# Modulation vectors as row sums on VectorE in a two-block fp32 kernel

## The chip, the cores and the metric

The kernel runs on one core of a Trainium2 chip. The metric is the device time of one execution in microseconds (us), taken as the median of several runs. TensorE (PE; PEld is its weight load) does matrix products, VectorE (DVE) and ScalarE (ACT) elementwise work, GpSimd (POOL) elementwise work and DMA issues, SyncE (SP) DMA issues alone. Each engine works through its own queue in order.

## The reference, cut to what matters

Two transformer-like blocks run one after the other on 256 latent tokens, the first (two layers) beside 256 context tokens, with features D = 1024. Each layer scales and shifts its normalised input by "modulation" vectors, which come from one condition vector through a matrix of 1024 x 6144:

```
s_lat = silu(c);  s_ctx = silu(c_ctx)                  # each [1024]
for l in range(2):
    ml = split(s_lat @ w_ada[l] + b_ada[l], 6)         # six vectors of 1024
    mc = split(s_ctx @ w_ada[l] + b_ada[l], 6)         # the same for the context
    hl = rmsnorm(xl, g) * (1 + ml[1]) + ml[0]          # needed first of all
    hc = rmsnorm(xc, g) * (1 + mc[1]) + mc[0]
    yl, yc = mixer(hl, hc)     # four mLSTM heads, eight differential attention heads, Fourier, gates
    xl = xl + ml[2] * yl       # from here on the other vectors
    xl = xl + ml[5] * swiglu(rmsnorm(xl, g2) * (1 + ml[4]) + ml[3])
    ...                        # the context likewise, in layer 0
```

The second block (HGRN2 and S5 mixers, then a product-key expert layer) has one such matrix too, `ada_w_2`, and one stream, `silu(c_2)`.

## The kernel before

**Products.** Activations are kept transposed, features on the 128 partitions and tokens along the row (512 columns: latent and context). A product in fp32 is made of three matmuls with operands split into a high and a low part: hi x hi, hi x lo, lo x hi (L217 to L219 for most products, L417 to L419 in `first_products`). The weights arrive by DMA as tiles of 128x1024 (`raw`), ScalarE casts the high part (`whi`, L171 or L189), VectorE takes the difference as the low part (`wlo`, L176 or L190; GpSimd in some products). Two products' worth of weights are in buffers, so the weights of one product are made ready during the one before.

**Work beside the products.** Attention steps, gates and the like are generators. `spend`, called at every product, takes one step of the first generator in `k.todo` (by `fill`) and, by a clock of estimated us, steps of those in `k.bg` (by `tick`):

```
    def fill(self):
        if self.todo:
            if next(self.todo[0], None) is None:
                self.todo.pop(0)
    ...
    def spend(self, us):
        self.fill()
        self.clock += us
        while self.clock >= self.step:
            self.clock -= self.step
            self.tick()
```

Inside the stretches that are scheduled by hand, which hold the modulation, the order on each engine is the order in which the program is written, that is, the order in which these steps are taken; each engine's queue is then fixed.

**Modulation before.** `ada_cond` (L274) makes `cs`, the silu of both conditions as columns [128, 8, 32]; a second one for block 2. `rounds` (L2075, in `block1`) puts six rounds for each of the three matrices into `k.todo`, 18 in all. A round (`ada_round`, L293) makes one vector of 1024 for its streams: for each of eight k it loads a tile of 128x1024 through SP's queue (L304, two buffers with the tag `ada`; the next load is issued in the step that uses the tile two before it), and lets it run through TensorE in four matmuls of 256 columns against `cs[:, k]` (L318, `pada<-ada,cs`). Then the row of results is copied (L323), turned into columns by two transposes (L326) and added to the bias (L335), which gives `ada` [128, streams, 48]. The first two vectors of layer 0, shift and scale of the first norm, are made together in two half rounds from sixteen loads each into buffers with the tag `yb` (L310).

**The start.** `first_products` (L400) makes the first norm and the first five products by halves of the features: k steps 0 to 3 of `affine_steps` (L428: `k`, L437, on VectorE; `h`, L450, on ScalarE; its low part, L452, on VectorE), then the products with these, then steps 4 to 7 and the products with those. Before each half, `mod` (L1043) makes `modA` from that half's modulation. `fill` is called beside the first half's products, and between the halves and after the second `fill_until(16)` empties `k.todo` down to 16 rounds.

Names in the rows: `pacc`, `ps`, `po`, `pada` are PSUM tiles, `x` the residual, `po` in L437 the rows of 1/rms, `e`, `den` attention scores and their row sums, `junk` a tile that nobody reads.

Of the kernel before, what the change touches and what calls it, by code (L numbers as in the profile page):

```python
# [13 lines left out]
AF = mybir.ActivationFunctionType  # L14
ALU = mybir.AluOpType
# [4 lines left out]
for _p, _t in {  # L20
    "C1": "ada adarow c_cosT c_sinT c_dft1 c_dftc c_dfts c_maskf c_maskb dakl craw1 craw2 cth",
    "P1": "q k v oth hn crow cdiag aT e0 e1 ropea ropeb gc h gb gb2 den den2 dast",
    "Y": "yb",
    "Rx": "x",
    "R2": "xl hl",
    "P2": "u",
}.items():
    for _n in _t.split():
        POOL_OF[_n] = _p
# [7 lines left out]
# products between two steps of the work beside them, by length: mLSTM, differential attention, Fourier  # L37
# [12 lines left out]
class K:  # L50
    def __init__(self, tc, d, ctx):
        self.tc, self.nc, self.d, self.ctx = tc, tc.nc, d, ctx
        self.pools = {}
        self.n = 0
        self.guards = {}
        self.bg = []
        self.clock, self.step = 0.0, 2.6
        self.todo = []
        self.ahead = []
        self.lines = None, None  # L60
        # whether GpSimd makes the low parts of the weights of a line
        self.spare = False
        # whether the steps beside a product come before its matrix products in the order, or after them
        self.early = False
# [18 lines left out]
    # ---- work that runs beside the products: generators, one step at a time between product tiles  # L83
# [3 lines left out]
    def tick(self):  # L87
        """one step of the first generator, and of those behind it that it lets start"""
# [29 lines left out]
    def pipe(self, rows):  # L118
        """rows of stages, each row one step behind the row before; the successor starts after the last row's first"""
# [6 lines left out]
    # ---- sections in the order given: the weights of each product are made ready during the one before  # L126
# [4 lines left out]
    def line(self, src, kt, product, after=None, us=0.0, split=False):  # L131
        """product(weights) comes with the next call; after(its result) one call later, in two parts (before and after
        the next weights, or half of them)"""
# [15 lines left out]
    def prepare(self, src):  # L149
        """the weights of the next line before its time"""  # L150
# [14 lines left out]
    # ---- products: every float32 operand is hi + lo, both float32r  # L165
# [30 lines left out]
    def gemm_t(self, acc, src, xs, cols, kt=KT):  # L196
        """acc[n, tok] = sum over k of w[k, n] x[k, tok]"""
        self.gemm_ts([(acc, src)], xs, cols, kt)

    def gemm_ts(self, jobs, xs, cols, kt=KT):  # L200
        """the same for several tiles, k by k: for an x that is still being made"""
# [19 lines left out]
    def gemm_m(self, accs, src, xs, tts):  # L221
        """[tok, 256 cols] = sum over k of x[k, tok] w[k, n], for the token tiles tts, two to a bank of accs;
        the first start of a bank clears it for both"""
# [14 lines left out]
    # ---- constants  # L238
# [13 lines left out]
    def more_consts(self):  # L252
# [16 lines left out]
        # low part of k of one head of the differential attention, for each map with zeros in the other map's rows  # L269
# [3 lines left out]
    # ---- modulation: silu(c) @ w + b, as one column of six vectors for each stream  # L273
# [11 lines left out]

    def ada_tile(self, name, bias, ns):
# [6 lines left out]
    def ada_round(self, cs, w, r, bt, out, ns, half=None):  # L293
        """columns r*1024 .. r*1024+1023 of the modulation, or the same half of each of its first two vectors;
        loads run as far ahead as there are buffers"""
        nc = self.nc
        wts = []

        def load():
            k = len(wts)  # L300
            if k < KT:
                if half is None:
                    wt = self.t([P, 1024], "ada", 2)
                    nc.sync.dma_start(wt, w[k * P:(k + 1) * P, r * 1024:(r + 1) * 1024])  # L304
                    wts.append((wt[:, :T2], wt[:, T2:]))
                else:
                    wts.append([self.t([P, T2], "yb", self.nyb) for _ in range(2)])
                    for v, wt in enumerate(wts[-1]):
                        c = v * 1024 + half * T2
                        nc.sync.dma_start(wt, w[k * P:(k + 1) * P, c:c + T2])  # L310

        for _ in range(2 if half is None else KT):
            load()
        yield "-"
        acc = self.ps("ada")
        for k in range(KT):
# [3 lines left out]
            load()  # L320
# [7 lines left out]
        def part(a):  # L328
            if half is None:
                return a[:, r * 8:(r + 1) * 8].rearrange("p (r j b) -> p r j b", r=2, j=2)  # L330
# [6 lines left out]
    # ---- rmsnorm over the features of x[k] = [128, tok]  # L337
    def sq_add(self, k, src, n, first=None, engine=None):
        """adds the squares of x[k] (and of x[k] * first beside them) to the sums over k"""
# [11 lines left out]
    def sq_cols(self, nt):  # L351
        """the sums over all features, tokens on partitions, a column for each 128"""
# [12 lines left out]
    def rows(self, rs, nt, tag="o", between=None):  # L365
        """columns of tokens to rows on every partition"""
# [8 lines left out]
    def halves(self, srcs):  # L375
        """the weights of pairs of products, first all those of the first half of the features, then of the second"""
# [23 lines left out]
    def first_products(self, accs, split, x, pr, mod, streams):  # L400
        """the first norm and the first products with it, by halves of the features: the second half of its modulation is
        made beside the products with the first. mod(half) gives A, B"""
# [25 lines left out]
    def affine_steps(self, x, pr, A, B, streams, pair, hs, early=0, ks=range(KT)):  # L428
        """x * pr * A + B, split; streams: [(columns, s)] with A[s], B[s] = [128, 8];
        one k a step, the first early of them begun before the first"""  # L430
# [25 lines left out]
    def sq_rows(self, nt, tag="o", work=None, between=None):  # L456
        """1 / rms of the tokens in rows"""
# [7 lines left out]
    # h = x * A / rms + B still lacks the rms when the first products with it are due: these take x * A instead,  # L465
    # with B in a further column: (w^T (x * A)) / rms + w^T B
# [11 lines left out]
    def raw_product(self, w, xs, tags, at=None, between=None):  # L478
        """one tile for each stream that has a tag"""
# [14 lines left out]
    def raw_finish(self, accs, rows, t, bias=True):  # L494
        """acc * rows + w^T B into t; without bias the columns w^T B are returned instead of added"""
# [12 lines left out]
    def norm_ahead(self, base, residual, x, A, B, srcs, tags, norm, finish, rpair, pair, at, follow, after_that,  # L508
                   first=None, close=None):
        """base: the products that end x, [(weights, kt, product, us)], with residual(k, acc); the squares of x are summed  # L510
        on the way, and norm = (columns, rows of 1 / rms). Beside that go the products of srcs with x * A, which
        finish(j, accs, rows) ends; follow() starts the next line, and the weights of the one after that are made ready.
        Returns h"""
# [42 lines left out]
        # h takes the place of x * A  # L556
# [15 lines left out]
    def follow(self, src):  # L572
        """the weights for the first product after a line"""
# [4 lines left out]
    # pairs (high, low) of split activations; with b further columns for each stream  # L578
# [18 lines left out]
    # ---- mLSTM  # L597
    def ml_gates(self, l, acc):
# [10 lines left out]
        # log sigmoid(f) = min(f, 0) - log1p(exp(-|f|)); log1p(e) = 2 atanh(e / (2 + e))  # L609
# [16 lines left out]
        # cumulative sums and maxima in each direction  # L626
# [30 lines left out]
    def ml_qkv(self, l, h, hs, need_ctx, qk):  # L657
        """q^T, k^T [128, 2, tok] and v [tok, 4, 256] of one head; qk: those made already"""
# [21 lines left out]
    def ml_o(self, l, h, hs, th):  # L680
        """tanh(o / 2) of one head"""
# [6 lines left out]
    def ml_head(self, l, h, qkv, th, g, tts, ys):  # L688
# [65 lines left out]
        # y = hn^T * g * (tanh(o/2) + 1); g holds head_g / 2  # L754
# [13 lines left out]
    def av(self, st, nk, vof, w, out):  # L768
        """stages of out[tok, w] = rmsnorm over w of A[tok, nk] @ v, with A = st["A"]"""
# [25 lines left out]
    # ---- differential attention  # L795
# [1454 lines left out]
```

## Time and profile before

| | |
|---|---|
| runs of the kernel before | 3129.56 us median of 3 (3129.42 to 3132.8) |
| the profiled execution | span 3129.0 us (the page gives no other time for it) |
| PE busy | 97% of the span |
| PEld busy | 86% |
| DVE busy | 62% |
| ACT busy | 43% |
| POOL busy | 14% |
| DMA | 153 GB/s in the mean |

The page divides the span among engines. TensorE is busy nearly throughout; whether another engine has room is a question of the stretch, so the rows further below are by stretch and by place.

### The profile page before, as it was taken

The page shows a single profiled execution, that of the slowest core. Times are in us where ns is not written, and L with a number is a line of the kernel's source. Part 1 is how long each engine was busy: PE and PEld are TensorE (multiplying, and loading weights), DVE is VectorE, ACT ScalarE, POOL GpSimd, SP SyncE. Part 2 cuts the span into 40 slices and gives each one's busy share as a digit, 9 for nine tenths or more (in the row PEclk, how much of TensorE's full clock was granted, in tenths as well). Part 3 has the DMA queues.
Part 4 walks back from the last instruction along what each step waited for, and adds up shares of the span by engine and source line. Part 5 has one row for each costly group of instructions (what it writes and reads, how often), then busy time and mean ns, then how long its engine had stood idle before and what let it go on. Part 6 is the DMA issues. An engine that isn't in the chain of part 4 may idle for free.

```text
span 3129.0 us, 53569 instructions
## 1 busy us (share of the span) xinstructions
PE 3036.7 (97%) x21466; PEld 2686.8 (86%) x21466; DVE 1940.2 (62%) x3643; ACT 1350.2 (43%) x2310; POOL 435.8 (14%) x524
## 2 busy tenths in 40 slices
PE   7999999999999999999999999997899999999998
PEld 4778777887787777788898999986799999999998
DVE  5544627653455333474568667689789778866665
ACT  3343425542233221344456545455554545444444
POOL 2101001101121000022001022684210000000000
PEclk9999999999999999999999999998999999999999
DMA  7443343324434434443242355552357765566665
GB/s 257 130 130 118 122 135 121 109 75 128 152 122 135 151 130 153 151 136 125 92 138 95 102 195 171 180 154 85 106 165 233 228 211 160 162 219 226 231 225 170
DMA packets 151034, 479.46 MB, mean 153 GB/s; under 512 B 19616, under 2 KB 23520, under 8 KB 150784
## 3 DMA queue, kind: packets, MB, share of 16 engines
q1 hardware_dynamic: 145296, 464.82, 45.8%
q0 software_dynamic: 2608, 7.55, 0.9%
q8 instruction: 168, 2.75, 0.4%
q10 hardware_dynamic: 2880, 3.67, 0.3%
q14 instruction: 82, 0.67, 0.1%
HBM read 457.85 MB, written 18.12 MB: 152 GB/s over the span
## 4 chain that ended last, share of the span: by engine, by line
issue 28%; PE 19%; DVE 5%; ACT 1%; POOL 1%; POOLq 0%; DVEq 0%; ACTq 0%
PE pacc L219 4%; PE pacc L217 4%; PE pacc L218 4%; PE pacc L235 1%; DVE wlo L176 1%; PE pacc L233 1%; PE pacc L234 1%; PE po L785 1%; DVE wlo L190 1%; DVE ropeb L819 0%; DVE hl L452 0%; PE ps L712 0%; POOL ssum L349 0%; PE pt L776 0%; ACT whi L171 0%
## 5 line engine op out<-in xcount | busy, mean ns | idle before, releaser
L176 DVE TENSOR_TENSOR wlo<-raw,whi 128x1024 fp32r<-128x1024 f32 x498 | 630.5, 1266 | 471.8 <-ACT whi L171 462.8
L171 ACT CAST whi<-raw 128x1024 fp32r<-128x1024 f32 x498 | 519.8, 1044 | 793.3 <-PE pacc L218 479.9
L217 PE MATMUL pacc<-h,whi 128*128 128x512 f32 (+1 forms) x1280 | 476.7, 372 | 0.0
L219 PE MATMUL pacc<-h,wlo 128*128 128x512 f32 (+1 forms) x1280 | 465.8, 364 | 1.9 <-DVE wlo L176 1.9
L219 PE MATMUL pacc<-hl,wlo 128*128 128x256 f32 x1600 | 454.2, 284 | 12.9 <-DVE wlo L176 10.6
L218 PE MATMUL pacc<-h,whi 128*128 128x512 f32 (+1 forms) x1280 | 461.1, 360 | 2.9 <-DVE h L452 2.9
L218 PE MATMUL pacc<-hl,whi 128*128 128x256 f32 x1600 | 454.2, 284 | 7.3 <-DVE hl L452 7.0
L217 PE MATMUL pacc<-hl,whi 128*128 128x256 f32 x1600 | 458.9, 287 | 0.6 <-ACT whi L171 0.3
L189 ACT CAST whi<-raw 128x1024 fp32r<-128x1024 f32 (+2 forms) x211 | 192.0, 920 | 418.7 <-PE pacc L218 285.7
L219 PEld LDWEIGHTS pacc<-hl,wlo 128*128 128x128 f32 x1600 | 304.6, 190 | 14.4 <-DVE wlo L176 11.2
L218 PEld LDWEIGHTS pacc<-hl,whi 128*128 128x128 f32 x1600 | 305.7, 191 | 10.3 <-DVE hl L452 9.7
L217 PEld LDWEIGHTS pacc<-hl,whi 128*128 128x128 f32 x1600 | 306.5, 192 | 1.9 <-ACT whi L171 0.8
L217 PEld LDWEIGHTS pacc<-h,whi 128*128 128x128 f32 x1280 | 240.9, 188 | 56.1 <-issue 18.7
L190 DVE TENSOR_TENSOR wlo<-raw,whi 128x1024 fp32r<-128x1024 f32 (+2 forms) x163 | 199.8, 1226 | 131.7 <-ACT whi L189 131.2
L219 PEld LDWEIGHTS pacc<-h,wlo 128*128 128x128 f32 x1280 | 240.5, 188 | 43.2 <-DVE wlo L176 3.0
L218 PEld LDWEIGHTS pacc<-h,whi 128*128 128x128 f32 x1280 | 241.0, 188 | 42.5 <-DVE h L452 4.4
L217 PE MATMUL pacc<-yb,whi 128*128 128x512 f32 (+1 forms) x624 | 230.4, 369 | 0.0
L219 PE MATMUL pacc<-yb,wlo 128*128 128x512 f32 (+1 forms) x624 | 225.6, 362 | 0.8 <-DVE wlo L176 0.7
L218 PE MATMUL pacc<-yb,whi 128*128 128x512 f32 (+1 forms) x624 | 225.5, 361 | 0.0
L233 PE MATMUL pacc<-whi,h 128*128 128x256 f32 x704 | 202.4, 288 | 0.0
L235 PE MATMUL pacc<-wlo,h 128*128 128x256 f32 x704 | 198.3, 282 | 1.7 <-POOL wlo L190 1.0
L234 PE MATMUL pacc<-whi,h 128*128 128x256 f32 x704 | 198.4, 282 | 0.9 <-DVE h L452 0.9
(587 smaller groups left out, 6352.2 us busy)
## 6 DMA issues: line engine op xcount, KB each, us to landing
ada<-in_w_ada_dram SPq DMA_DIRECT2D x128, 512.0 KB, 3.9
raw<-in_peer_u_dram SPq DMA_DIRECT2D x128, 512.0 KB, 4.0
raw<-in_peer_v_dram SPq DMA_DIRECT2D x128, 512.0 KB, 3.8
raw<-in_w_f_dram SPq DMA_DIRECT2D x120, 512.0 KB, 3.6
raw<-in_w_gp_dram SPq DMA_DIRECT2D x48, 512.0 KB, 3.5
spill<-k SPq DMA_DIRECT2D x61, 256.0 KB, 4.3
k<-spill SPq DMA_DIRECT2D x61, 256.0 KB, 2.6
raw<-in_w_out_dram SPq DMA_DIRECT2D x24, 512.0 KB, 3.4
```

The lines of the kernel that those rows point to most:

```text
L171: nc.scalar.copy(hi, raw)
L176: self.nc.vector.tensor_sub(lo, raw, hi)
L189: self.nc.scalar.copy(hi, raw)
L190: (self.nc.gpsimd if self.spare else self.nc.vector).tensor_sub(lo, raw, hi)
L217: nc.tensor.matmul(acc, hi[:, k], xh[:, cols], start=k == first, stop=False)
L218: nc.tensor.matmul(acc, hi[:, k], xl[:, cols], start=False, stop=False)
L219: nc.tensor.matmul(acc, lo[:, k], xh[:, cols], start=False, stop=(k + 1) % kt == first)
L233: nc.tensor.matmul(a, xh[:, s], hi[:, k], start=half + k == 0 and not sk, stop=False, skip_group_check=sk)
L234: nc.tensor.matmul(a, xl[:, s], hi[:, k], start=False, stop=False, skip_group_check=sk)
L235: nc.tensor.matmul(a, xh[:, s], lo[:, k], start=False, stop=half * 4 + k == 7, skip_group_check=sk)
L785: nc.tensor.matmul(po[:, :w], aT[:, s * P:(s + 1) * P], vof(s), start=s == 0, stop=s == nk // P - 1)
```

## The change

The two half rounds at the start stay as they are (now `ada_half`, with their weights in an array of their own, `w_ada0`). Sixteen rounds, ten for two streams and six for one, change their form. The matrices are handed over transposed, so that a tile of 128x1024 has one output feature on each partition and all 1024 input features along its row. The conditions come as raw rows, broadcast to all partitions by the DMA (`cb`, once for block 1 and once for block 2), and are made into `(tanh(c/2) + 1) * c` there. VectorE then multiplies a tile by that row and by 0.5 and adds up along the row in the same instruction (L316), one for each tile and stream; the products go to `junk`, the sum straight into its column of `ada`. No PSUM tile, copy or transpose is left in these rounds. The loads still go through SP, with the same two buffers and the same size. The Tanh results of the conditions lie in these buffers too (`th`), in the first step of the first such round.

Comments are taken out as well, which moves line numbers: L437, L452 and L1043 before are L460, L475 and L1066 after, L729 and L731 are L752 and L754. `dynamic_dma_scratch_size=4096` is new in the constructor of the program.

```diff
+    def ada_rows(self, src, ns):
+        nc = self.nc
+        cb = self.t([P, 2, D], "cb", 1)[:, :ns]
+        nc.scalar.dma_start(cb, bass.AP(tensor=src.tensor, offset=src.offset, ap=[[0, P], [D, ns], [1, D]]))
+        for s in range(ns):
+            th = self.t([P, D], "ada", 2)
+            nc.scalar.activation(th, cb[:, s], AF.Tanh, scale=0.5)
+            nc.vector.scalar_tensor_tensor(cb[:, s], th, 1.0, cb[:, s], op0=ALU.add, op1=ALU.mult)
+        return cb
+
+    def ada_sums(self, rows, w, r, bt, out, ns):
+        nc = self.nc
+        wts = []
+        def load():
+            j = len(wts)
+            if j < KT:
+                wts.append(self.t([P, D], "ada", 2))
+                nc.sync.dma_start(wts[j], w[j])
+        if rows[0] is None:
+            rows[0] = self.ada_rows(rows[1], ns)
+        cb = rows[0]
+        for _ in range(2):
+            load()
+        yield "-"
+        for j in range(KT):
+            for s in range(ns):
+                nc.vector.scalar_tensor_tensor(self.junk, wts[j], 0.5, cb[:, s], op0=ALU.mult, op1=ALU.mult,
+                                               accum_out=out[:, s, 8 * r + j:8 * r + j + 1])
+            load()
+            yield "-"
+        v = slice(8 * r, 8 * r + 8)
+        for s in range(ns):
+            nc.vector.tensor_add(out[:, s, v], out[:, s, v], bt[:, v])
...
-    def ada_round(self, cs, w, r, bt, out, ns, half=None):
+    def ada_half(self, cs, w, half, bt, out, ns):
...
-                    wt = self.t([P, 1024], "ada", 2)
-                    nc.sync.dma_start(wt, w[k * P:(k + 1) * P, r * 1024:(r + 1) * 1024])
-                    wts.append((wt[:, :T2], wt[:, T2:]))
...
-    cs2 = k.ada_cond(d["cT2"], 1, "2", nc.gpsimd)
+    k.junk = k.t([P, D], "junk", 1)
...
-            k.todo.append(k.ada_round(c, w, r, bt, out, ns, r if l == 0 and r < 2 else None))
+            if l == 0 and r < 2:
+                k.todo.append(k.ada_half(cs, d["w_ada0"], r, bt, out, ns))
+            else:
+                k.todo.append(k.ada_sums(rows, d["w_ada"][l, r], r, bt, out, ns))
-    rounds(0, cs, 2, d["w_ada"][0], d["ada_b"][0])
+    rows = [None, d["c_rows"]]
+    rounds(0, rows, 2, d["ada_b"][0])
...
-    rounds(1, cs, 2, d["w_ada"][1], d["ada_b"][1])
-    rounds(2, cs2, 1, d["w_ada2"], d["ada_b2"])
+    rounds(1, rows, 2, d["ada_b"][1])
+    rounds(2, [None, d["c_rows"][2:]], 1, d["ada_b2"])
...
+    w = np.concatenate([i["w_ada"], i["ada_w_2"]])
+    o["w_ada"] = f(w.transpose(0, 2, 1).reshape(3, 6, KT, P, D))
+    o["c_rows"] = f(np.stack([i["c"][0], i["c_ctx"], i["c_2"][0]]))
```

What the change does to the order of the queues is shown at three places.

VectorE at the first norm, between its two halves, before (`k` and `h` are its k steps, L323 and L335 end the second half round):

```order
L323 COPY k_106_428<-pada_340 128x256
L335 TENSOR_TENSOR ada_16_111<-pada_340,adab_15_109 128x2x4 x2
L1043 SCALAR_TENSOR_TENSOR modA_84_288<-ada_16_111,ng_150 128x4 x2
L437 SCALAR_TENSOR_TENSOR k_111_456<-x_79,modA_84_288,po_225 128x256 x2
L452 SCALAR_TENSOR_TENSOR h_460<-k_111_456,ada_16_111,h_459 128x256 x2
L437 SCALAR_TENSOR_TENSOR k_114_465<-x_81,modA_84_288,po_225 128x256 x2
L452 SCALAR_TENSOR_TENSOR h_469<-k_114_465,ada_16_111,h_468 128x256 x2
L437 SCALAR_TENSOR_TENSOR k_119_478<-x_83,modA_84_288,po_225 128x256 x2
```

and with the change:

```order
L294 SCALAR_TENSOR_TENSOR cb_433<-ada_435,cb_433 128x1024
L294 SCALAR_TENSOR_TENSOR cb_433<-ada_438,cb_433 128x1024
L316 SCALAR_TENSOR_TENSOR junk_95,ada_14_104<-ada_441,cb_433 128x1024 x2
L1066 SCALAR_TENSOR_TENSOR modA_82_281<-ada_14_104,ng_143 128x4 x2
L316 SCALAR_TENSOR_TENSOR junk_95,ada_14_104<-ada_443,cb_433 128x1024
L460 SCALAR_TENSOR_TENSOR k_111_454<-x_79,modA_82_281,po_218 128x256 x2
L316 SCALAR_TENSOR_TENSOR junk_95,ada_14_104<-ada_443,cb_433 128x1024
L475 SCALAR_TENSOR_TENSOR h_458<-k_111_454,ada_14_104,h_457 128x256 x2
L460 SCALAR_TENSOR_TENSOR k_114_463<-x_81,modA_82_281,po_218 128x256 x2
L316 SCALAR_TENSOR_TENSOR junk_95,ada_14_104<-ada_450,cb_433 128x1024
L475 SCALAR_TENSOR_TENSOR h_467<-k_114_463,ada_14_104,h_466 128x256 x2
```

Between the second half's modulation and its first k step there now stand the two products that make `cb`, three row sums (L316) on two tiles, `ada_441` and `ada_443`, and `modA`; each later k step has a row sum in it.

ScalarE at the same place, with the change (L189 are casts of weights, L473 is `h` of the k steps, L290 the issue of the conditions' load):

```order
L473 ACTIVATE h_321<-k_95_318,ada_14_104 128x256 x2
L189 CAST whi_368<-raw_174 128x512
L189 CAST whi_414<-raw_259 128x1024
L290 DMA cb_433<-in_c_rows_dram 128x2048
L293 ACTIVATE ada_435<-cb_433 128x1024
L293 ACTIVATE ada_438<-cb_433 128x1024
L473 ACTIVATE h_457<-k_111_454,ada_14_104 128x256 x2
L473 ACTIVATE h_466<-k_114_463,ada_14_104 128x256 x2
```

The issue and two activations of 1024 columns are new there, ahead of the second half's first `h`.

VectorE at the last of the mLSTM heads, where the attention begins, in the stretch from 69 to 372 us, before (`wlo` are low parts of weights, `hn`, `ms` a head's output and its norm, `k`, `e`, `den` attention):

```order
L788 TENSOR_SCALAR ms_2248<-ms_2248 128x1
L791 TENSOR_SCALAR hn_1858<-po_2243,msr_2251 128x256
L176 TENSOR_TENSOR wlo_2397<-raw_2393,whi_2395 128x1024
L176 TENSOR_TENSOR wlo_2460<-raw_2456,whi_2458 128x1024
L760 SCALAR_TENSOR_TENSOR k_453_2359<-oth_1813,pt_2354 128x512
L729 SCALAR_TENSOR_TENSOR e_464_2386,den_2427<-ps_2383,e_464_2386 128x128
L731 SCALAR_TENSOR_TENSOR e_465_2387,den_2427<-ps_2383,e_465_2387 128x256
L735 SCALAR_TENSOR_TENSOR den_471_2430<-den_2427 128x2
```

and with the change, at the same products:

```order
L811 TENSOR_SCALAR ms_2206<-ms_2206 128x1
L316 SCALAR_TENSOR_TENSOR junk_95,ada_72_270<-ada_3951,cb_433 128x1024
L814 TENSOR_SCALAR hn_1825<-po_2201,msr_2209 128x256
L316 SCALAR_TENSOR_TENSOR junk_95,ada_72_270<-ada_3951,cb_433 128x1024
L322 TENSOR_TENSOR ada_72_270<-ada_72_270,adab_71_268 128x8 x2
L316 SCALAR_TENSOR_TENSOR junk_95,ada_72_270<-ada_4261,cb_433 128x1024 x2
L176 TENSOR_TENSOR wlo_2347<-raw_2343,whi_2345 128x1024
L316 SCALAR_TENSOR_TENSOR junk_95,ada_72_270<-ada_4263,cb_433 128x1024 x2
L316 SCALAR_TENSOR_TENSOR junk_95,ada_72_270<-ada_4349,cb_433 128x1024
L783 SCALAR_TENSOR_TENSOR k_449_2309<-oth_1778,pt_2304 128x512
L752 SCALAR_TENSOR_TENSOR e_460_2336,den_2375<-ps_2333,e_460_2336 128x128
L754 SCALAR_TENSOR_TENSOR e_461_2337,den_2375<-ps_2333,e_461_2337 128x256
```

Four row sums and two additions now stand between `ms` and the next low part, and three more ahead of the attention's steps.

TensorE at the start of the second half's products, before (`pacc` and `ps` are products of the first norm):

```order
L417 MATMUL ps_287<-h_328,whi_375 128x512
L418 MATMUL ps_287<-h_329,whi_375 128x512
L419 MATMUL ps_287<-h_328,wlo_376 128x512
L318 MATMUL pada_447<-ada_440,cs_11_91 32x256 x4
L417 MATMUL pacc_283<-h_459,whi_421 128x512
L418 MATMUL pacc_283<-h_460,whi_421 128x512
L419 MATMUL pacc_283<-h_459,wlo_422 128x512
```

and with the change:

```order
L440 MATMUL ps_280<-h_321,whi_368 128x512
L441 MATMUL ps_280<-h_322,whi_368 128x512
L442 MATMUL ps_280<-h_321,wlo_369 128x512
L440 MATMUL pacc_276<-h_457,whi_414 128x512
L441 MATMUL pacc_276<-h_458,whi_414 128x512
L442 MATMUL pacc_276<-h_457,wlo_415 128x512
```

The matmuls on the tile `ada` (L318) are gone; the products stand in the same order.

## Rows read from the trace of the kernel before

**Rows 1.** Busy time by stretch (of the engines PE, PEld, DVE, ACT, POOL), granted clock, DMA share, GB/s.
```profile
69.00:372.00 303.00, 301.04 (x1718) 237.56 (x1717) 159.15 (x354) 119.38 (x241) 32.85 (x46) 1.00 0.40 124
...
480.00:960.00 480.00, 472.71 (x2802) 384.36 (x2801) 258.19 (x512) 194.34 (x391) 74.48 (x86) 1.00 0.37 118
960.00:1300.00 340.00, 337.13 (x1637) 250.22 (x1638) 130.34 (x187) 82.28 (x106) 2.68 (x2) 0.99 0.44 146
```

**Rows 2.** Line L318: all its matmuls on modulation tiles, and its share of one stretch.
```profile
L318 PE MATMUL pada<-ada,cs x1024: 379/379/404, 49.4 to 1341.5; 128*32 128x256 f32 x171
...
69.00:372.00 303.00, 18.50 (x224) 4.54 (x224) 1.00 0.40 124
```

**Rows 3.** Timeline of TensorE at a tile and at transposes (start, us, engine, what).
```profile
1034.96 0.39 PE L218 MATMUL pacc<-h,whi 128*128 128x512 f32 x1
1035.20 0.40 PE L219 MATMUL pacc<-h,wlo 128*128 128x512 f32 x1
1035.52 0.64 PE L318 MATMUL pada<-ada,cs 128*32 128x256 f32 x8
1036.09 0.51 PE L217 MATMUL pacc<-yb,whi 128*128 128x512 f32 x1
...
751.33 0.39 PE L219 MATMUL pacc<-yb,wlo 128*128 128x512 f32 x1
751.56 0.38 PE L326 MATMUL pada<-c_ident,k 128*128 128x128 f32 x2
751.69 0.48 PE L217 MATMUL pacc<-h,whi 128*128 128x512 f32 x1
```

**Rows 4.** VectorE from 69 to 372 by line and form; its timeline at a sum.
```profile
L176 DVE TENSOR_TENSOR wlo<-raw,whi 128x1024 fp32r<-128x1024 f32 x41 | 50.1, 1223 | 88.5 <-ACT whi L171 85.0 <-PE po L785 3.5
...
116.90 0.69 DVE L731 SCALAR_TENSOR_TENSOR e<-ps,e 128x512 f32<-128x512 f32 x1
117.51 0.08 DVE L731 DVE_READ_ACCUMULATOR e<-ps,e 128x1 f32 x1
117.63 0.16 DVE L735 SCALAR_TENSOR_TENSOR den<-den 128x2 f32<-128x2 f32 x1
```

**Rows 5.** Timeline of ScalarE and VectorE at the first norm's second half and the gates.
```profile
45.53 1.05 ACT L189 CAST whi<-raw 128x1024 fp32r<-128x1024 f32 x1 [8.02 <-PE ps L418]
...
49.18 0.87 DVE L437 SCALAR_TENSOR_TENSOR k<-x,modA,po 128x256 f32<-128x256 f32 x2
50.23 0.89 DVE L452 SCALAR_TENSOR_TENSOR h<-k,ada,h 128x256 fp32r<-128x256 f32 x2 [0.18 <-ACT h L450]
...
67.99 1.23 DVE L176 TENSOR_TENSOR wlo<-raw,whi 128x1024 fp32r<-128x1024 f32 x1 [5.65 <-ACT whi L171]
69.13 0.41 DVE L614 TENSOR_SCALAR yb<-yb 64x512 f32<-64x512 f32 x1
69.58 3.35 DVE L615 RECIPROCAL yb<-yb 64x512 f32<-64x512 f32 x1
```

**Rows 6.** Timeline of TensorE there: second half's first product, last k step's first, last product.
```profile
50.65 0.50 PE L417 MATMUL pacc<-h,whi 128*128 128x512 f32 x1 [0.62 <-ACT h L450]
...
58.64 0.50 PE L417 MATMUL pacc<-h,whi 128*128 128x512 f32 x1
...
68.25 0.40 PE L419 MATMUL ps<-h,wlo 128*128 128x512 f32 x1
```

**Rows 7.** DMA: tile ada from issue to landing; another size, from the page's issues.
```profile
DMA to landing us min/median/max: 3.6/3.9/8.2
...
k<-spill SPq DMA_DIRECT2D x61, 256.0 KB, 2.6
```

**Rows 8.** Busy time in two short stretches with the fullest VectorE (columns as in 1).
```profile
560.00:580.00 20.00, 17.09 (x98) 12.52 (x97) 18.33 (x41) 11.18 (x26) 4.24 (x5) 1.00 0.38 118
...
1380.00:1400.00 20.00, 19.69 (x128) 16.82 (x127) 19.57 (x37) 7.76 (x13) 0.00 (x0) 1.00 0.58 184
```

**Rows 9.** Line L803: products of two SBUF operands with an accumulator.
```profile
L803 DVE SCALAR_TENSOR_TENSOR k<-k x4: 217/219/220, 58.5 to 59.2; 128x64 f32<-128x64 f32 x4
```

More of the change, by code (lines that the diff above doesn't have):

```diff
@@ L20 @@
 for _p, _t in {
-    "C1": "ada adarow c_cosT c_sinT c_dft1 c_dftc c_dfts c_maskf c_maskb dakl craw1 craw2 cth",
+    "C1": "ada cb junk c_cosT c_sinT c_dft1 c_dftc c_dfts c_maskf c_maskb dakl craw1 craw2 cth",
     "P1": "q k v oth hn crow cdiag aT e0 e1 ropea ropeb gc h gb gb2 den den2 dast",
@@ L291, in ada_tile @@
         return bt, out
-    def ada_round(self, cs, w, r, bt, out, ns, half=None):
+    def ada_half(self, cs, w, half, bt, out, ns):
         nc = self.nc
         wts = []
[L299 to L302, printed above, removed]
-                    wt = self.t([P, 1024], "ada", 2)
-                    nc.sync.dma_start(wt, w[k * P:(k + 1) * P, r * 1024:(r + 1) * 1024])
-                    wts.append((wt[:, :T2], wt[:, T2:]))
[L306 to L313, printed above, removed]
+        for k in range(KT):
+            wts.append([self.t([P, T2], "yb", self.nyb) for _ in range(2)])
+            for v, wt in enumerate(wts[-1]):
+                c = v * 1024 + half * T2
+                nc.sync.dma_start(wt, w[k * P:(k + 1) * P, c:c + T2])
         yield "-"
@@ L319, in ada_round @@
                                  start=k == 0, stop=k == KT - 1)
-            load()
             yield "-"
@@ L328, in part @@
         def part(a):
-            if half is None:
-                return a[:, r * 8:(r + 1) * 8].rearrange("p (r j b) -> p r j b", r=2, j=2)
             return a[:, :16].rearrange("p (r h j b) -> p h r j b", r=2, h=2, j=2)[:, half]
@@ L2073, in block1, with rounds @@
     k.todo = []
-    def rounds(l, c, ns, w, b):
+    def rounds(l, rows, ns, b):
         bt, out = k.ada_tile(str(l), b, ns)
@@ L2139, in layout1 @@
     o["cT"] = f(np.stack([cols8(i["c"][0]), cols8(i["c_ctx"])], -1))
[L2140 removed]
+    o["w_ada0"] = f(i["w_ada"][0][:, :2048])
+    w = np.concatenate([i["w_ada"], i["ada_w_2"]])
+    o["w_ada"] = f(w.transpose(0, 2, 1).reshape(3, 6, KT, P, D))
+    o["c_rows"] = f(np.stack([i["c"][0], i["c_ctx"], i["c_2"][0]]))
     o["ada_b"] = f(cols8(i["b_ada"]))
@@ L2234 @@
     from concourse.bass_utils import run_bass_kernel_spmd as _run
-    nc = _bacc.Bacc("TRN2", target_bir_lowering=False, num_devices=1)
+    nc = _bacc.Bacc("TRN2", target_bir_lowering=False, num_devices=1, dynamic_dma_scratch_size=4096)
     laid = layout1(inputs)
```

3 lines of the change are left out of this document (removed).

## Prediction

> **What bounds the kernel now.** I read the busy time by stretch first, then the timeline at single places, then the DMA landings. From 69 to 372 us, the four mLSTM heads and the first differential attention, TensorE is busy 301.0 of 303 us and VectorE 159.2; from 480 to 960 it is 472.7 of 480 against 258.2, from 960 to 1300 337.1 of 340 against 130.3 [rows 1]. TensorE sets the time there, VectorE has room in the mean. The modulation runs in this half of the program alone: 1024 matmul records (128 tiles of 4 matmuls, two passes each) from 49.4 to 1341 us [rows 2].
>
> What a tile costs TensorE is read from starts, since records overlap. Between two matmuls of a product 0.23 to 0.24 us pass; with a tile's eight between them 0.89 us (1035.20 to 1036.09), so a tile adds 0.66 us [rows 3]. The pair of transposes that ends a round adds 0.36 - 0.23 = 0.13 us, at 751.33 to 751.69 [rows 3].
>
> **The change part by part.** *Removed from TensorE:* 128 x 0.66 = 85 us and 16 x 0.13 = 2 us, nearly all in stretches where it is full: **-87 us** if nothing else waits. The two half rounds at the start keep their matmuls.
>
> *Added to VectorE:* two streams have 10 rounds of 8 tiles between them, block 2 has 6 rounds for one: 160 + 48 = 208 row sums of 128x1024. No row has this form. The nearest of its length is the weights' low part, 1.22 us [rows 4], with the next instruction 1.14 us behind (67.99 to 69.13) [rows 5]. The nearest of its kind is a sum with accumulator over 512: 0.61 us from its start to the accumulator's read, 0.73 us to a dependent instruction [rows 4]. Another 512 elements at the rate at which 1024 take 1.14 (and 512 0.61), some 0.53 us, give 1.14 to 1.26 us. I take **1.2 us** with the read, as half of them follow another row sum: 250 us in all. The round's copies and additions that go, and the additions that come, are a few us off the path.
>
> *Where these land* is the point. The changed order does not spread them as the matmuls were spread. Counted in VectorE's order, 11 row sums stand before the first full-width low part of the weights (at 67.99 now), 119 between that and the 41st (370 now), 38 in the next 16 products, then none until about 960; the last 40 lie thinly in 960 to 1280, where VectorE has 210 us free [rows 1] for some 48: those cost nothing.
>
> *The start.* Both streams' conditions come as rows on every partition, 1 MB, issued by ScalarE behind the cast that starts at 45.53 [rows 5]. 256 KB land in 2.6 us, 512 KB in 3.9 (3.6 to 8.2) [rows 7]; 1.3 us for each further 256 KB makes 6.5 us, so 52.1. Then one after the other: a Tanh of 1024 columns (1.05 like the cast), the product with it (1.2), only now a weight load, whose buffers the Tanh results held (3.9 and 0.3 of issue): 58.6. Two row sums, modA, a third row sum (4.0): 62.6. Only behind these stand the k steps of the second half of the norm, because VectorE takes its queue in order, and the half's first matmul, 1.5 us behind the first k step's start (49.18 to 50.65), starts at 64.1 instead of 50.65 [rows 5, 6]. Each later k step carries a row sum, 0.87 + 0.89 + 1.2 = 3.0 us against (58.64 - 50.65) / 3 = 2.7, so the last begins near 73.5 instead of 58.64. The products end near 83 instead of 68.5 (68.25 is the last's start) [rows 6]. The first low part now has behind the last k step four row sums, a reciprocal of 3.35 [rows 5] and small ones ahead of it, and is ready near 87 instead of 69.2: 18 us later, in spite of three tiles of matmuls less (2 us, counted above). Against the -87 the start costs **+20 us**; 17 with the load at 4 us, 28 with both loads at 8.2.
>
> *69 to 372.* VectorE: 159 + 119 x 1.2 = 302 us, less some 2 for the round's copies: 300. TensorE: 303 less 28 tiles (224 records [rows 2] / 8) x 0.66 and the transposes: 284. So the engine with room in the mean is now the longer one, by **+16 us**; 9 at 1.14, 23 at 1.26. This is the step on which the sign hangs: the cover (144 us free) is used up by the 143 us laid on it.
>
> *How full a VectorE can get.* It waits for casts, attention results and loads. Where it is fullest now it still idles 0.4 of 20 us (1380 to 1400) or 1.7 of 20 (560 to 580) [rows 8], 2 to 8% of 300 us: 6 to 25. On top comes a wait of its own: a tile's load is issued when the row sums of the tile two before it are done, and between them and its own row sums the order puts 2.8 to 9 us of other work in this stretch, under 4.3 us (landing and issue) 15 times, 10 us short in sum. In the 560 window TensorE idled 2.9 of 20 us, 15%, which is 45 us over the stretch: the upper bound. I take **+25 us** for all, the middle.
>
> *Small ones.* Block 2's condition row is one more load and Tanh on ScalarE with a cast of weights behind them: 4 + 1 us, of which a product of 5.6 us covers all or nothing; and in 480 to 960 TensorE idled 7.3 us [rows 1], so not all of a tile may come back there. **+4 us**, 0 to 10. After 480 us nothing is added until 960, and the gain of some 87 tiles stands.
>
> *Sum:* 3129.0 - 87 + 20 + 16 + 25 + 4 = **3107 us**. The span is 0.6 us under the median of the runs, which I leave out. By the lower ends 3129 - 87 + 17 + 9 + 6 = 3074, by the upper 3129 - 87 + 28 + 23 + 45 + 10 = 3148.
>
> *A rule of the Trainium skill* speaks against the change. In the rows, a product of two fp32 operands in SBUF with accumulator takes 0.219 us for 64 columns [rows 9], an instruction of 2 columns 0.16 [rows 4]: 0.06 us for 62 columns, one a cycle at the rate of the long ones. The Trainium skill, Vector Engine (DVE) Microarchitecture Reference, section 7 (Points that are easy to get wrong), says that this kind of instruction with two sources in SBUF that aren't bf16 runs at half throughput, as no read port is left for the accumulator. The row disagrees, but it is 64 columns long, so the rule stands below as a rival.
>
> **The rivals.**
> 1. *VectorE keeps step.* It idles as in 1380 to 1400 and the waits for loads fall into waits for casts: 3129 - 87 + 18 + 12 + 8 + 0 = 3080. For it: TensorE waited for VectorE hardly at all before, 2 of 303 us idle [rows 1]. Against: fewer than 1% spare in that stretch, two products' worth of weight buffers.
> 2. *Loads at the head of VectorE's queue* (slower). Place: 69 to 430. A row sum waits for its tile and holds the low parts and attention steps behind it; SyncE, in order, holds the next weights behind a tile's load that waits for its buffer. Price: 48 us short in sum at 6 us from issue to landing, 86 at 7 (by the distances in the order). In place of the 10 us above, 7 us gives 3107 + 76 = 3183, and from about 5.8 us on nothing is gained. For it: single landings took 8.2 [rows 7], and the tiles come nearly twice as fast there. Against: the median was 3.9, and the DMA engines were busy 0.40 [rows 1].
> 3. *Half throughput.* 2.25 us each: 119 x 1.05 = 125 us more in 69 to 372, some 40 in the next products, less the idle time that it swallows, and 8 at the start: 3107 + 150 = 3257. By the Trainium skill's rule named above; [rows 9] against it.
> 4. *Nothing moves:* start and idle time at their upper ends, 3123 to 3136. That the matmuls stay is excluded by the changed order, which has none after the first two vectors.
>
> **How the numbers follow.** A measurement of this kernel can tell about 0.2%, 6 us, from no change. The forecast has 0.62, its own range 3086 to 3136: 0.48 faster, 0.11 within 0.2%, 0.03 slower. Rival 1 has 0.16 (faster), rival 2 0.17 and rival 3 0.02 (slower), rival 4 0.03 (no change). So faster 0.64, same 0.14, slower 0.22. The range, 3074 to 3148, goes from the lower to the upper ends of the sum; it leaves out rival 3, most of rival 2 and the edge of rival 1, under 0.2.
>
> **What would show it.** Row sums of 1.15 to 1.3 us with their read, 208 of them. The second half's first product near 64 us, TensorE idle some 14 us before it. From 85 to 430 us VectorE busy over 90% and TensorE at 85 to 92%, with waits of its matmuls for low parts of the weights in place of none. From 430 to 960 and 960 to 1300 shorter by 0.66 us a tile. I am wrong if TensorE stays above 97% in 85 to 430 (rival 1), if VectorE's longest waits there end with loads of ada tiles (rival 2), if a row sum takes 2 us (rival 3), or if the later stretches don't shrink.

## The result and the profile after

The changed kernel takes 3165.82 us (median of 4, 3162.39 to 3166.9), the kernel before beside it 3130.68; the ratio is 1.0109, 95% interval 1.0095 to 1.0123. So it is **slower by 1.1%**; the forecast was 3107 us, faster, and the range ended at 3148. The profiled execution has a span of 3165.1 us. The page's first two parts:

```profile
PE 2984.3 (94%) x20410; PEld 2690.3 (85%) x20410; DVE 2169.6 (69%) x4043; ACT 1350.7 (43%) x2312; POOL 450.6 (14%) x523
...
PE   6999999999998888899999999998799999999998
...
DVE  5999987754364434475467767779779878866665
```

TensorE's busy time fell by 52 us and VectorE's rose by 229, yet the span grew by 36. The 40 slices are 79 us each: the 13th to 17th of TensorE (949 to 1345 us) are at 8, where it had 337 of 340 us before [rows 1].

To place it I paired the k-th matmul of both traces, all that write `pada`, and so the modulation's, left out (19,262 remain in each), and took the difference of their starts: how far the changed kernel is behind.

| place in the kernel before, us | behind, us | change over the stretch | tiles of matmuls gone, 0.66 each |
|---|---|---|---|
| 46 | -1.0 | | |
| 69 | 13.1 | +14.1 | |
| 372 | 20.5 | +7.4 | 28: 18.5 |
| 480 | 12.3 | -8.2 | 10: 6.6 |
| 960 | -12.5 | -24.8 | 39: 25.9 |
| 1300 | 42.9 | **+55.4** | 40: 26.5 |
| 1400 | 36.6 | -6.3 | 8: 5.3 |
| end | 36.4 | -0.2 | |

Until 960 the change was on its way to a gain. From there to 1300, layer 0's feed-forward products with block 2's row sums beside them, the time went up by 55 us where 26 should have come off: **82 us lost in one stretch**, the one where I had counted nothing. Busy time there (columns as in [rows 1]), with the two places ahead of it:

```profile
82.00:391.50 309.50, 287.09 (x1487) 236.77 (x1486) 288.27 (x597) 118.00 (x240) 49.37 (x46) 0.98 0.54 174
...
496.40:947.60 451.20, 440.29 (x2473) 378.06 (x2474) 256.15 (x496) 191.78 (x390) 72.47 (x86) 1.00 0.25 82
947.60:1345.10 397.50, 344.19 (x1317) 260.84 (x1318) 172.97 (x263) 83.71 (x108) 3.04 (x5) 0.93 0.35 124
```

The last line answers to 960 to 1300 in [rows 1]. TensorE is busy 344 of 397.5 us, VectorE only 173: no engine is full, and the granted clock is 0.93 in the mean. From 82 to 391 us, on the other hand, VectorE is at 288 of 309.5: full, as forecast. TensorE's longest waits there (85 to 372 us; who waited for whom: us in total, times, longest) are for steps of the heads and the attention; none of its waits is for a low part of the weights:

```profile
PE ps L890 <- ACT e L895: 4.7, 1, 4.7
PE pt L781 <- DVE k L783: 3.7, 1, 3.7
```

A row sum takes what I took for it (shortest, median, longest, ns):

```profile
L316 DVE SCALAR_TENSOR_TENSOR junk<-ada,cb x208: 1204/1218/2614, 56.5 to 1307.5; 128x1024 f32<-128x1024 f32 x104
```

The waits of 960 to 1340, in the same form, those of the engines first, then SyncE's queue:

```profile
ACT whi L189 <- DMA raw<-in_w_f_dram: 207.4, 32, 9.2
DVE wlo L190 <- ACT whi L189: 181.7, 43, 7.8
...
PE pacc L217 <- ACT whi L189: 38.0, 26, 2.8
```

```profile
SPq L306 <- DVE junk L316: 295.3, 38, 23.9
```

TensorE waits for the cast of weights, the cast for the weights' load, and the load stands in SyncE's queue behind a tile's load (L306) that waits 295 us in sum for row sums. One turn of it, in the timeline of one product:

```profile
1207.94 1.22 DVE L316 SCALAR_TENSOR_TENSOR junk<-ada,cb 128x1024 f32<-128x1024 f32 x1
...
1209.08 0.08 DVE L316 DVE_READ_ACCUMULATOR junk<-ada,cb 128x1 f32 x1
...
1209.19 0.33 SPq L306 DMA_DIRECT2D ada<-in_w_ada_dram  x1
...
1209.61 0.38 SPq L184 DMA_DIRECT2D raw<-in_w_f_dram  x1
...
1212.43 0.39 PE L219 MATMUL pacc<-h,wlo 128*128 128x512 f32 x1
1213.85 1.04 ACT L189 CAST whi<-raw 128x1024 fp32r<-128x1024 f32 x1 [7.17 <-DMA raw<-in_w_f_dram]
...
1214.92 1.23 DVE L190 TENSOR_TENSOR wlo<-raw,whi 128x1024 fp32r<-128x1024 f32 x1 [5.76 <-ACT whi L189]
...
1214.95 0.50 PE L217 MATMUL pacc<-yb,whi 128*128 128x512 f32 x1 [2.13 <-ACT whi L189]
...
1216.66 1.22 DVE L316 SCALAR_TENSOR_TENSOR junk<-ada,cb 128x1024 f32<-128x1024 f32 x1
...
1217.81 0.08 DVE L316 DVE_READ_ACCUMULATOR junk<-ada,cb 128x1 f32 x1
```

The row sum (L316) ends at 1209.16 with its accumulator's read; 0.03 us later SyncE issues the next tile's load, and at 1209.61 the next product's weights. These land 4.2 us later, the cast (1.04) follows at 1213.85, the low part (1.23) at 1214.92, and behind that on VectorE a step of the feed-forward and the next row sum, which ends at 1217.9. That is a **ring of 8.7 us**: weights' load, cast, low part, row sum, and through SyncE's order the next weights' load. The 24 matmuls of a product take 5.6. TensorE stands from 1212.8 to 1214.95. No link of it is new work on a full engine. Before, the tile's buffer was freed by matmuls, which lie ahead of a product and not behind its low part: SyncE waited 212 us for them (960 to 1300 there), yet the cast waited only 15 us for its load.

```profile
SPq L304 <- PE pada L318: 211.9, 30, 19.1
```

```profile
ACT whi L189 <- DMA raw<-in_w_f_dram: 15.2, 3, 5.4
```

At the start (ScalarE, VectorE, SyncE and TensorE; before in [rows 5, 6]):

```profile
44.55 0.34 ACTq L290 DMA_DIRECT2D cb<-in_c_rows_dram  x1
...
49.25 2.00 ACT L293 ACTIVATE ada<-cb 128x1024 f32<-128x1024 f32 x2 [3.69 <-DMA cb<-in_c_rows_dram]
...
50.34 2.36 DVE L294 SCALAR_TENSOR_TENSOR cb<-ada,cb 128x1024 f32<-128x1024 f32 x2 [2.06 <-ACT ada L293]
...
52.58 0.82 SPq L306 DMA_DIRECT2D ada<-in_w_ada_dram  x2
...
56.48 1.23 DVE L316 SCALAR_TENSOR_TENSOR junk<-ada,cb 128x1024 f32<-128x1024 f32 x1 [3.77 <-DMA ada<-in_w_ada_dram]
...
57.74 1.23 DVE L316 SCALAR_TENSOR_TENSOR junk<-ada,cb 128x1024 f32<-128x1024 f32 x1
...
58.90 0.23 DVE L1066 SCALAR_TENSOR_TENSOR modA<-ada,ng 128x4 f32<-128x4 f32 x2
...
59.05 1.22 DVE L316 SCALAR_TENSOR_TENSOR junk<-ada,cb 128x1024 f32<-128x1024 f32 x1
...
60.19 0.86 DVE L460 SCALAR_TENSOR_TENSOR k<-x,modA,po 128x256 f32<-128x256 f32 x2
...
60.98 1.21 DVE L316 SCALAR_TENSOR_TENSOR junk<-ada,cb 128x1024 f32<-128x1024 f32 x1
...
61.66 0.80 PE L440 MATMUL pacc<-h,whi 128*128 128x512 f32 x1 [13.20 <-ACT h L473]
```

The chain is the forecast's: load, Tanh, product, weight load, three row sums with `modA` among them, k step. The half's first matmul starts at 61.66 instead of 50.65; 64.1 was said.

### The profile page after: what moved, and what is told of

It reads as the page before. It is cut to its first block, busy times and chain, and to the rows that moved or that the text cites. A ratio compares the mean times of both kernels' runs of the same rounds, so it can differ in the third digit from the quotient of the medians.

```text
span 3165.1 us, 51932 instructions
## 1 busy us (share of the span) xinstructions
PE 2984.3 (94%) x20410; PEld 2690.3 (85%) x20410; DVE 2169.6 (69%) x4043; ACT 1350.7 (43%) x2312; POOL 450.6 (14%) x523
## 5 line engine op out<-in xcount | busy, mean ns | idle before, releaser
L217 PE MATMUL pacc<-h,whi 128*128 128x512 f32 (+1 forms) x1280 | 480.3, 375 | 28.3 <-ACT whi L189 27.7
L219 PE MATMUL pacc<-h,wlo 128*128 128x512 f32 (+1 forms) x1280 | 473.7, 370 | 10.0 <-DVE wlo L190 8.2
L218 PE MATMUL pacc<-h,whi 128*128 128x512 f32 (+1 forms) x1280 | 472.2, 369 | 3.1 <-DVE h L475 3.0
L219 PE MATMUL pacc<-hl,wlo 128*128 128x256 f32 x1600 | 455.8, 285 | 12.3 <-DVE wlo L176 10.6
L189 ACT CAST whi<-raw 128x1024 fp32r<-128x1024 f32 (+2 forms) x211 | 192.0, 920 | 465.8 <-DMA raw<-in_w_f_dram 207.4
L219 PEld LDWEIGHTS pacc<-hl,wlo 128*128 128x128 f32 x1600 | 306.2, 191 | 13.8 <-DVE wlo L176 11.2
L217 PEld LDWEIGHTS pacc<-h,whi 128*128 128x128 f32 x1280 | 245.9, 192 | 77.7 <-ACT whi L189 35.5
L218 PEld LDWEIGHTS pacc<-h,whi 128*128 128x128 f32 x1280 | 246.2, 192 | 44.1 <-DVE h L475 4.4
L316 DVE SCALAR_TENSOR_TENSOR junk<-ada,cb 128x1024 f32<-128x1024 f32 x208 | 259.1, 1246 | 18.5 <-DMA ada<-in_w_ada_dram 17.1
L217 PE MATMUL pacc<-yb,whi 128*128 128x512 f32 (+1 forms) x624 | 229.7, 368 | 10.2 <-ACT whi L189 10.2
L233 PE MATMUL pacc<-whi,h 128*128 128x256 f32 x704 | 202.0, 287 | 2.0 <-ACT whi L171 2.0
```

Of the source, the lines that this page charges most:

```text
L189: self.nc.scalar.copy(hi, raw)
L217: nc.tensor.matmul(acc, hi[:, k], xh[:, cols], start=k == first, stop=False)
L218: nc.tensor.matmul(acc, hi[:, k], xl[:, cols], start=False, stop=False)
L219: nc.tensor.matmul(acc, lo[:, k], xh[:, cols], start=False, stop=(k + 1) % kt == first)
L233: nc.tensor.matmul(a, xh[:, s], hi[:, k], start=half + k == 0 and not sk, stop=False, skip_group_check=sk)
L316: nc.vector.scalar_tensor_tensor(self.junk, wts[j], 0.5, cb[:, s], op0=ALU.mult, op1=ALU.mult, accum_out=out[:, s, 8 * r + j:8 * r + j + 1])
```

## The experiments

Three theories of the lost 82 us: **A**, the ring through SyncE's order; **B**, VectorE's own 1.2 us more ahead of what TensorE waits for; **C**, more bytes for the DMA engines at a time. For 69 to 480 us: **V**, a full VectorE; **S**, the loads' order. Each kernel's distance behind the kernel before, by the same pairing:

| kernel | at 69 | 372 | 480 | 960 | 1300 | 1400 | 1700 | end | 960 to 1300 takes |
|---|---|---|---|---|---|---|---|---|---|
| the change | 13.1 | 20.5 | 12.3 | -12.5 | 42.9 | 36.6 | 37.0 | 36.4 | 395 |
| load one tile ahead | 15.2 | 22.0 | 14.4 | -10.2 | -42.4 | -48.7 | -48.4 | -45.7 | 308 |
| short row sums | 9.1 | 26.4 | 18.7 | -8.3 | 16.1 | 9.8 | 9.7 | 10.2 | 364 |
| GpSimd's queue | 16.3 | 23.5 | 18.4 | -4.9 | -37.2 | -43.5 | -43.7 | -42.7 | 308 |
| block 2 as matmuls | 13.1 | 20.0 | 11.9 | -9.1 | -7.7 | -13.5 | -13.5 | -15.5 | 341 |
| conditions early | -1.7 | 5.3 | 5.9 | -19.9 | 31.6 | 25.3 | 24.9 | 24.7 | 391 |
| early + one ahead | -0.7 | 6.3 | 6.3 | -17.7 | -50.1 | -56.4 | -56.5 | -55.7 | 307 |
| one ahead + held | 13.8 | 6.7 | -1.0 | -28.2 | -59.4 | -45.4 | -30.9 | -31.0 | 309 |
| all three | -0.4 | -8.9 | -16.6 | -43.5 | -74.8 | -59.9 | -44.3 | -44.9 | 309 |
| all three, held at 9 | 1.3 | 4.5 | -3.2 | -30.1 | -61.2 | -62.3 | -52.8 | -51.0 | 309 |

**Load one tile ahead.**

```diff
-        for _ in range(2):
-            load()
+        load()
         yield "-"
         for j in range(KT):
+            load()
             for s in range(ns):
                 nc.vector.scalar_tensor_tensor(self.junk, wts[j], ...
-            load()
```

> A tile's load is written ahead of the row sums of the tile before it, one tile ahead instead of two: same two buffers, same bytes, same order on VectorE, but SyncE's queue now waits for row sums that ended a product earlier. Theory A, a loop through SyncE's order (weights' load 4.2 us, cast 1.04, low part 1.2, other VectorE work, row sum 1.2, only then the next weights' load: some 8.7 us a product against 5.6 of matmuls): the products that took 340 us at 960 to 1300 before and 395.6 with the change take 314 to 320; 372 us and less after them; total 3085 us (3075 to 3095). Theory B, the row sums' own 1.2 us on VectorE ahead of low parts: nothing of that changes, total 3160 to 3168. Theory C, the DMA engines are shared by more bytes at a time: nothing changes either, 3160 to 3168.

3082.84 us, ratio to before 0.9844 (0.9827 to 0.986). A: 83 us gone, all of them between 960 and 1300, by moving the place where a tile's load is written. B and C are out: row sums, bytes and VectorE's order there are the same. Its stretch (950 to 1261 us), the casts' waits and SyncE's in it:

```profile
950.00:1261.00 311.00, 308.14 (x1322) 249.08 (x1321) 175.65 (x263) 83.48 (x107) 3.59 (x6) 0.99 0.45 156
```

```profile
ACT whi L189 <- PE pacc L218: 201.5, 50, 4.5
...
ACT whi L189 <- DMA raw<-in_w_f_dram: 5.4, 1, 5.4
```

```profile
SPq L306 <- DVE junk L316: 188.1, 38, 15.5
```

SyncE still waits 188 us for row sums, and it costs nothing: the cast now waits for matmuls to free its buffers, and once, for 5.4 us, for a load, instead of 207 us in 32 waits. How long a queue waits says little; what stands behind the wait, and when that is due, says it.

**Short row sums.**

```diff
-nc.vector.scalar_tensor_tensor(self.junk, wts[j], 0.5, cb[:, s], ...
+nc.vector.scalar_tensor_tensor(self.junk[:, :64], wts[j][:, :64], 0.5, cb[:, s, :64], ...
```

> Each row sum takes 64 of the 1024 columns (the other 960 features are left out of the modulation vectors), so it takes 0.22 us instead of 1.22; loads, waits and queues stay. Theory A: the loop shortens by 1.0 to 7.7 us, still 2.1 of 3.1 us over a product: the stretch that takes 395.6 us with the change takes about 369; with some 20 us from a less full VectorE in 85 to 372 us the total is 3119 us. Theory B: the stretch takes 314 and the total is 3066. Theory C: the stretch stays at 395, total 3146.

3135.8 us, ratio 1.0011 (1.0001 to 1.002). The stretch takes 364 us, near A's 369 and far from B's 314 and C's 395: the ring is shorter by the missing microsecond and still too long. The total missed all three, for 69 to 372 us became worse, not better, with VectorE busy only 183 of 322 us:

```profile
78.00:400.00 322.00, 293.59 (x1495) 241.06 (x1496) 182.93 (x688) 119.64 (x246) 33.32 (x46) 0.97 0.63 206
```

In place of the full engine came another wait; VectorE's waits for tiles there (85 to 372), in this kernel and in the changed one:

```profile
DVE junk L316 <- DMA ada<-in_w_ada_dram: 87.2, 50, 5.0
```

```profile
DVE junk L316 <- DMA ada<-in_w_ada_dram: 5.1, 8, 1.5
```

With short sums the scheduler, which orders this part, brings the tiles still closer together (the first 168, those of both layers and of block 2's first round, stand ahead of the 33rd full-width low part, not the 56th), and VectorE stands 87 us for loads, with attention steps behind. That is the first half of rival 2's mechanism, seen. In the changed kernel it is 5 us in 8 waits: there VectorE is full instead.

**GpSimd's queue.**

```diff
-                nc.sync.dma_start(wts[j], w[j])
+                nc.gpsimd.dma_start(wts[j], w[j])
```

> The tiles' loads are issued by GpSimd instead of SyncE, still two tiles ahead and still behind the row sums that free their buffers. Theory A, SyncE's order is what carries the wait on to the weights: the stretch of 395.6 us falls to 314 to 320 as with the load one tile ahead, though the distance of the loads is the old one; GpSimd does nothing else there. In 85 to 480 us GpSimd's own steps may now wait behind such an issue, for 0 to 30 us. Total 3080 to 3115. Rival: it is the distance of two tiles that costs, on whichever queue (the row sum comes late for its own next load): the stretch stays near 395 and the total near 3160.

3087.58 us, 0.9862 (0.9842 to 0.9882). With the old distance of two tiles the stretch takes 308 us, as with one: it was the queue that the wait stood in. By 480 us it is 6 us behind the changed kernel, from which it differs in the queue alone; 3 of them stand there at 69 already.

**Block 2 as matmuls** (its six rounds as `ada_round` was, from the untransposed matrix).

> Block 2's six rounds as matrix products again, the ten rounds for two streams as row sums. All theories: if the loss lies in block 2's 40 tiles at 960 to 1300 of before, that stretch takes 340 us again and the kernel ends at 3130 - 12 = 3118 us (the change stood 12.4 us ahead at 960). If the loss there comes from something else (a later order of work, the clock), the stretch stays over 380 us and the total over 3150.

3118.73 us, 0.9961 (0.9947 to 0.9975): as expected. The other ten rounds alone are worth some 12 us.

**Conditions early.**

```diff
+        rows[0] = k.cb0 = k.ada_rows(d["c_rows"], 2)   # behind the first half round
...
+            if half == 0:
+                self.ada_silu(self.cb0, 2)             # Tanh into junk, behind the first half's k steps
...
-                    if half == 0:
+                    if half == 0 and len(self.todo) > 16:
                         self.fill()
```

> The conditions' rows are loaded before the first norm's first half, their Tanh lands in the junk tile instead of the tiles' buffers, and no row sum is put ahead of the second half. If the chain load, Tanh, product, weight load, row sums is what held the second half's first matmul (63.6 us with the change, 51.5 before), that matmul starts at 50 to 52 and the total falls by 12 to 15, to 3152 us. Rival: VectorE at 93% in 85 to 372 us takes the same work a little later, and by 480 us less than 5 us are left of the gain: 3161 to 3166.

3154.25 us, 1.0077 (1.006 to 1.0094). The half's first matmul starts earlier than before the change (two later matmuls stand in the expectation; by this row it is 61.66 and 50.65):

```profile
48.92 0.50 PE L447 MATMUL pacc<-h,whi 128*128 128x512 f32 x1 [1.19 <-ACT h L480]
```

Of 14.8 us gained at 69, 11.7 are left at the end. **Both** (conditions early, load one tile ahead):

> Load one tile ahead and the conditions early, together. If the two costs are separate: 3083 - 12 = 3071 us (3066 to 3076). If the 14 us of the start come back as waiting for VectorE in the stretch behind it: 3078 to 3084.

3075.16 us, 0.9822 (0.9806 to 0.9839), together with the last one below the fastest here. The two costs are nearly separate: 7.7 of the 12 us came.

**Later rounds held back.** `fill` stops at 12 rounds left while layer 0's attention is written, so 64 row sums stand there instead of 168:

```diff
     def fill(self):
-        if self.todo:
+        if len(self.todo) > self.held:
```

> Load one tile ahead, and layer 1's and block 2's rounds are held back until layer 0's attention is written, so 64 row sums instead of 168 stand in 69 to 480 us. Theory V, a full VectorE (93% in 85 to 372 us) with row sums ahead of attention steps swallowed the 25 us of matmuls that went there: at 480 of before the kernel is 0 to 10 us ahead instead of 15 behind, at 960 some 30 ahead, and the total is 3062 to 3072. Theory S, the loads' order on SyncE or the start alone set that stretch: it stays 12 to 15 us behind at 480, total 3080 to 3085.

> All three: load one tile ahead, conditions early, later rounds held back. With theory V and separate costs 3130 - 87 + 2 to 15, 3045 to 3058 us; with theory S 3068 to 3075.

3102.04 us (0.9915, 0.9898 to 0.9931) and 3086.91 us (0.9865, 0.9849 to 0.9882): by the totals neither theory, by the places V. At 480 the first is 1 us ahead, where 168 row sums left it 14 behind, and all three together stand 75 us ahead at 1300. The tiles' loads fell with the row sums, so this alone does not exclude S; against S stands that the load one tile ahead, which changed SyncE's waits there too, gained nothing between 69 and 480. Behind 1300, 30 us are lost. Two stretches of the kernel with all three:

```profile
85.00:372.00 287.00, 275.64 (x1415) 226.59 (x1414) 213.06 (x462) 118.57 (x248) 42.60 (x47) 0.99 0.38 123
...
1240.00:1400.00 160.00, 143.01 (x837) 123.10 (x837) 134.53 (x242) 68.93 (x128) 46.81 (x47) 0.95 0.64 213
```

From 85 to 372 VectorE is at 213 of 287 and TensorE at 275.6 (266 in the change). From 1240 to 1400 VectorE is at 134.5 of 160 and TensorE at 143: the steps of the held rounds did not fit beside layer 0's feed-forward products, the rest was written in one go behind them, and block 2's row sums then stood among layer 1's heads and attention. So the last kernel held only from 9 rounds left:

> As all three together, but three of layer 1's six rounds stay in layer 0's attention, so that its feed-forward part has room for the other three and half of block 2's, and nothing is bunched behind it. If what all three lost behind 1340 us (75 us ahead there, 45 at the end) is the bunching and block 2's row sums crowding layer 1's start, the kernel is 60 to 70 us ahead at 1340 and still 55 to 65 at the end: 3066 to 3076 us. If any row sums of block 2 in layer 1's attention cost that, it falls to 45 ahead again, 3086.

3077.99 us, 0.9825 (0.9809 to 0.9842), 2 us over the first case. At 1300 and 1400 it stands 61 and 62 us ahead as expected, so the bunching is gone; 11 us go again by the end, 9.5 of them between 1400 and 1700, where the last 11 of block 2's row sums stand. By the places both had their part; no run tells the two apart.

## Why the prediction was wrong

- **The step that failed** is the last sentence on where the row sums land: "the last 40 lie thinly in 960 to 1280, where VectorE has 210 us free [rows 1] for some 48: those cost nothing". They cost 82 us. I compared VectorE's free time with its new work, the test for an engine's load, but a row sum also ends a tile's use, and so decides when SyncE goes on. I named that link, "SyncE, in order, holds the next weights behind a tile's load that waits for its buffer", and in the sum gave it a place only where VectorE is busy. It needs no busy VectorE: it needs the row sum to stand behind the low part of the very weights whose successors wait. The sum came out 59 us too low: 82 in that stretch, less some 25 by which the start, 69 to 480 and the small waits had been taken too high (below). Without these errors the miss would have been larger.
- *Rival 2* (0.17) had the second half of the mechanism, SyncE's order, at the wrong place (69 to 430) and by the wrong condition (landings of 6 us and more). No row sum waited for its tile in 960 to 1340, and the landings were 3.4 us for tiles and 4.4 for the weights there.
- *The start*: +20 forecast, less 2 for three tiles; 14.1 measured. The conditions' load took 4.7 us from issue to Tanh, 6.5 were taken.
- *69 to 480*: 16 + 25 = 41 us of cost forecast against 25 of matmuls gone; 24 measured (-0.8 us over both stretches). VectorE was full as said (93%), row sums waited for tiles 5 us in sum, 10 were taken. The 25 for waits were too many: TensorE was at 94% from 85 to 430 (323 of 345 us), not 85 to 92%. And its waits ended with steps of the heads and the attention, not with low parts of the weights, as had been said.
- *480 to 960*: -25 us for 39 tiles, as said; no row sum stands there.
- *A row sum* of 1.22 us with a read of 0.08, to the next start 1.24 to 1.26: as taken (1.2). The rule of the Trainium skill (Vector Engine (DVE) Microarchitecture Reference, section 7, half throughput for this kind) does not hold in these rows: the low part, with two such operands and no accumulator, takes the same 1.22 us [rows 4]. Rival 3 is out.
- *The order.* That it is the written one in all stretches with modulation was wrong from the mLSTM heads to the end of the mixers: there the kernel closes its manual schedule (`self.order.close()`, until `self.ordered()`), and a scheduler of the language orders the instructions. The numbers in the names count tiles as they are written, and `ada_3951` stands ahead of `wlo_2347` in the order of the changed kernel: its row sums were brought forward past 1,600 tiles. So they came twice as fast there as the matmuls had (119 row sums, some 60 tiles, from 69 to 372, against 28). The counts taken from the order were right.

With the ring open and all else as in the change the kernel ran 3083 us, under the sum's 3107: some 17 us of it from 69 to 480, and 10 more since in the stretch of the failed step 40 tiles gave 32 us (340 to 308), 0.8 each and not 0.66, and the 4 us for small waits were not needed; 3 us went again behind 1400.

## What to carry to other kernels

When a buffer's last reader moves to another engine, follow the buffer, not only the work: which queue waits for its release, what stands behind the wait there, and whether the new reader itself stands behind something that this queue delivers. If so, the loads in that queue run ahead by no more than one turn of the ring, whatever the engines' shares say. Here a load written ahead of the reader of the present tile opened it at no cost that the runs show; a queue of its own opened it too, for some us more at 480.

## What was not expected of the hardware

TensorE's clock fell behind some short gaps. In the ring's stretch TensorE idled 53 us in 54 gaps of at most 2.8 us (by the ends of its matmuls, which the profile models), against 3 us with the ring open. Its busy time for the same matmuls is longer too, by 36 us (344 against 308); together that is the 87. The granted clocks, 0.93 over 397.5 us against 0.99 over 311, account for at most some 25 of the 36 (28 less 3); where the rest comes from stays open. Around the turn shown above:

```profile
1206.00:1214.90 8.90, 6.07 (x24) 4.35 (x24) 2.97 (x4) 1.73 (x4) 0.00 (x0) 1.00 0.33 118
1214.90:1218.80 3.90, 3.45 (x8) 2.41 (x9) 3.57 (x5) 0.76 (x2) 0.00 (x0) 0.56 0.00 0
1218.80:1223.00 4.20, 3.97 (x17) 2.87 (x16) 0.69 (x1) 0.53 (x2) 0.00 (x0) 1.00 0.71 250
```

Full (2.4 GHz) ahead of the gap of 2.1 us, 0.56 in the mean of the 3.9 us behind it, near the lower level (1.2 GHz), then full again. So 50 us more of waiting came with 36 us more of matmuls.

VectorE's instructions grew beside some of GpSimd's: 7 of 208 row sums took 1.6 to 2.6 us, all of them beside GpSimd's work on whole tiles, as this one:

```profile
65.34 2.61 POOL L190 TENSOR_TENSOR wlo<-raw,whi 128x1024 fp32r<-128x1024 f32 x1 [17.30 <-ACT whi L189]
...
66.42 2.61 DVE L316 SCALAR_TENSOR_TENSOR junk<-ada,cb 128x1024 f32<-128x1024 f32 x1
```

GpSimd's subtraction began first; the row sum ends at 69.03, 1.08 us after the subtraction's end (67.95), little less than the 1.22 it takes alone. In all seven GpSimd's instruction had begun first; where the row sum had (at 127.19, 195.62, 255.80 and 335.28 us), it kept its 1.21 to 1.23 us. The Trainium skill, SBUF — State Buffer, SBUF: two separate sides, says that an instruction of VectorE with two operands in SBUF and one of GpSimd that reads SBUF exclude each other on a shared pair of ports, and that whichever starts first holds it to its end; these rows agree. Beside GpSimd's 128x1 steps (L813) none grew. The cost is small here: 7 row sums of 208, some 6 us.

The change's `dynamic_dma_scratch_size` was not tried by itself.
